# One kernel, its first stage and its heads: head 0's v of half 0 is computed first, two blocks of z behind the first stage, and each head's last chunk is turned in squares

## The chip, the cores and the metric

The kernel runs on one core of a Trainium2 chip. A core has engines with instruction queues of their own, which meet only through semaphores: TensorE (PE; matmuls, with weight loads as PEld), VectorE (DVE), ScalarE (ACT), GpSimd (POOL) and SyncE (SP, which here only issues DMAs). The metric is the device time of one launch in microseconds (us), lower is better. Before the change three runs gave 2084.30, 2090.53 and 2091.62 us.

## The reference

A trunk of two layers over 1024 tokens of width 1024. Only layer 0, gated linear attention with 4 heads, is touched; layer 1 is sparse attention with a top-k.

```python
h = x @ w_in                                    # (1024, 1024) @ (1024, 6160): q, k, v, z, a
g = log_sigmoid(a @ w_a2 + b_a) / 16            # a has 16 columns
# per head, chunk of tokens by chunk:
G = cumsum(g);  q_t = q * exp(G) / 16;  k_t = k * exp(-G)
o = tril(q_t @ k_t.T) @ v + (q * exp(G) / 16) @ S
S = S * decay + k_s.T @ v
# after all heads:
o = o * rsqrt(mean(o * o) + eps) * gn_g         # per head
y = (o * silu(z)) @ w_out
x = layer_norm(alpha * x + y);  x = x + (p @ ple_w) * sigmoid(x @ w_gate)
```

q and k have 256 columns per head, v and z 512. All of it is float32.

## The kernel before

Each float32 operand of a matmul is split into a high part (ScalarE copies it, rounded) and a low part (VectorE subtracts the high part), and each product is three matmuls: high by high, high by low, low by high. A block of 128 output columns over all 1024 inputs and 512 tokens is 24 matmuls of 512 columns. The work is one program order for each engine. The Python code keeps a count of TensorE time (`fl.now`, from the columns of the matmuls that it has written) and a heap of steps with due times; between matmuls it writes the steps that are due into the queues of the other engines. Nothing is reordered on the chip: what is written behind a waiting instruction on an engine waits too.

The tokens are done in two halves of 512. The first stage (`front_phase`) computes q, k and z for both halves in 15 pairs of blocks, with Strassen's seven products in place of eight: `products(1)` to `products(7)` are 12 matmuls each and need sums of parts of x (`T1` to `T5`, made once by `first_sums`, `t3`, `high`, `low`) and of weights (made for each pair by `steps`, `more_steps`, `last_steps`). Such preparing steps stand in `queue`, which `pace` empties by a gap, and which `todo` empties at once where a matmul needs a step. The stage opens with blocks 14 and 15 of z for half 0 (`z_first`), 48 matmuls in plain form, while the sums are made. The second half of x reaches the sums through a copy in DRAM (`xs`, then `load_T`).

Then each half of layer 0 runs. `v_phase(u, X)` computes v of one head, 96 matmuls into four PSUM banks, three of tag `pb` and one called `vT` that shares its bank with `oT`. For half 1 blocks 14 and 15 of z follow the first `v_phase`. Then for each head there is a core (`core_steps`, 16 steps over four chunks of 128 tokens) spread over bulk matmuls, which are the output product of the head before (`out_phase`, 96 matmuls) and v of the head behind (`v_phase`). In a core, `s1(c)` makes the scores (`tr`), `s2(c)` the update of the state (`U`), `s3(c)` the output of the chunk (`o`), and `s4(c)` turns that output and multiplies it by z. There are two ways to turn: by four transposes on TensorE into `oT`, or by squares (`by_square(c)`: 32x32 transposes on VectorE, four DMAs to DRAM and one back in `squares_out`, then `gate`). Before, chunks 0 to 2 of heads 0 to 2 go by squares, and chunk 3 by TensorE; head 3 has two chunks (three in half 1) by squares. A head's loop ends when its `s3(3)` is written (`fl.need(lambda: u.get("late"))`); `out_phase` reads the turned chunks in order.

`g_prep` prepares the next head while a core runs: it loads the gate's weights (`g_load`, on SP), splits them (`g_split`), and `g_phase` does two matmuls into `U` and a chain of ScalarE and VectorE steps on them (absolute value, exponential, logarithm, running sums, two more exponentials), then `qk_phase` multiplies q and k. The first `s1` of a head needs the end of that chain. `Weights` loads and splits plain blocks of weights in the order of `seq`, up to `W.stop`; `W.pace` writes one quarter of a split every 1.15 us of `fl.now`. `split_ahead` splits weights of the later layers in the background.

## Time and profile before

| | us |
|---|---|
| runs | 2084.30, 2090.53, 2091.62 (median 2090.53) |
| the profiled execution | 2087.2 |
| its span, first to last instruction | 2085.1 |
| PE busy | 1940.2 (93%) |
| DVE busy | 1553.6 (75%) |
| ACT busy | 968.8 (46%) |
| mean granted TensorE clock | 0.967 of 2.4 GHz |

TensorE is busy nearly throughout from 1100 us on, and the idle time lies before that. The stages are: the first stage from 0 to about 363.5 us, half 0 of layer 0 to about 640 with its tail to 780, half 1 from there to about 1100, then layer 1. A busy engine in these views may run at the lower clock: a matmul of 512 columns then takes about twice as long. A wait in brackets is the idle time of the engine just before the instruction, and names what ended it.

### The profile page before, as it was taken

What the parts mean: (1) busy time and instruction counts of PE and PEld (TensorE: products, weight loads), DVE (VectorE), ACT (ScalarE), POOL (GpSimd) and SP (SyncE); (2) the same over time, 40 slices, a digit from 0 to 9 for tenths busy, and PEclk for the clock granted to TensorE, in tenths of its full rate; (3) what the DMA queues carried; (4) which work ended last, traced back from release to release, by engine and by line L of the source; (5) the groups of instructions that cost most, each with busy time, mean ns of one, the idle gap of its engine ahead of it and who ended that gap; (6) DMA issues with size and microseconds to landing.
All of it is one profiled execution on the core that took longest, in us unless ns stands there. A gap on an engine that the chain in (4) does not pass through costs nothing.

```text
span 2085.1 us, 26854 instructions
## 1 busy us (share of the span) xinstructions
PE 1940.2 (93%) x8764; PEld 1592.4 (76%) x8764; DVE 1553.6 (75%) x3138; ACT 968.8 (46%) x1852; POOL 304.2 (15%) x568
## 2 busy tenths in 40 slices
PE   7799998878989998789859999999999999999999
PEld 5577887657768887667648888888878888888877
DVE  5677666577788686777886798777779787777873
ACT  3233443555455463444315467676642453434432
POOL 0023333133333202222202000000000000000000
PEclk8899999989999999999979999999999999999999
DMA  5268787889986987678617758887786898888874
GB/s 204 95 241 276 279 280 268 317 271 324 327 308 224 327 276 270 219 275 318 214 58 268 280 166 300 288 275 282 245 302 220 309 341 285 296 300 299 301 290 141
DMA packets 197195, 550.44 MB, mean 264 GB/s; under 512 B 25280, under 2 KB 38592, under 8 KB 190912
## 3 DMA queue, kind: packets, MB, share of 16 engines
q1 hardware_dynamic: 156640, 412.91, 58.0%
q0 software_dynamic: 40416, 135.82, 17.7%
q8 instruction: 69, 1.13, 0.2%
q14 instruction: 70, 0.57, 0.1%
HBM read 359.76 MB, written 190.97 MB: 264 GB/s over the span
## 4 chain that ended last, share of the span: by engine, by line
PE 55%; DVE 10%; DMA 7%; issue 6%; ACT 3%; POOL 1%; SPq 1%; DVEq 0%; ACTq 0%; POOLq 0%
PE pb L59 39%; PE o L59 6%; PE S L59 6%; DMA uf<-od 2%; PE U L59 1%; DMA wa2f<-in_g_a 1%; DMA wlo<-wls 1%; DVE tkj L1122 1%; DMA od<-ot 1%; DVE m L511 1%; DMA wls<-pst 1%; DVE y L811 1%; DVE v L420 1%; DVE bn L855 1%; DVE pst L251 0%
## 5 line engine op out<-in xcount | busy, mean ns | idle before, releaser
L59 PE MATMUL pb<-x,whi 128*128 128x512 f32 x1552 | 487.4, 395 | 11.2 <-DVE v L420 6.1
L59 PE MATMUL pb<-whi,u 128*128 128x512 f32 x1024 | 350.5, 403 | 5.9 <-DVE u L753 2.9
L59 PEld LDWEIGHTS pb<-x,whi 128*128 128x128 f32 x1552 | 286.4, 190 | 66.4 <-DVE v L420 6.5
L59 PE MATMUL pb<-x,wlo 128*128 128x512 f32 x776 | 305.2, 393 | 4.2 <-DVE wlo L1397 4.2
L59 PEld LDWEIGHTS pb<-whi,u 128*128 128x128 f32 x1024 | 198.4, 194 | 50.2 <-DVE u L753 4.3
L59 PE MATMUL pb<-wlo,u 128*128 128x512 f32 x512 | 204.2, 399 | 0.7 <-DMA wlo<-wls 0.7
L59 PEld LDWEIGHTS pb<-x,wlo 128*128 128x128 f32 x776 | 146.9, 189 | 37.8 <-DVE wlo L1397 5.9
L1906 ACT ACTIVATE sq<-P,mx 128x128 f32<-128x128 f32 (+7 forms) x128 | 98.9, 773 | 90.0 <-DVE mx L1899 70.0
L248 ACT ACTIVATE phi<-pst 128x512 fp32r<-128x512 f32 x130 | 81.3, 625 | 117.0 <-DMA pst<-in_d_z 26.4
L59 PE MATMUL pb<-whi,x 128*128 128x512 f32 x384 | 131.1, 395 | 3.8 <-DVE y L811 2.4
L849 POOL TENSOR_SCALAR rstd<-mv 128x1 f32<-128x1 f32 x16 | 5.8, 365 | 842.2 <-DVE mv L858 839.4
L59 PE MATMUL S<-kT,q 128*128 128x512 f32 (+2 forms) x576 | 122.7, 342 | 0.0
L251 DVE TENSOR_TENSOR pst<-pst,phi 128x512 fp32r<-128x512 f32 x130 | 88.8, 683 | 37.6 <-ACT phi L248 37.6
L1952 ACT ACTIVATE ph<-PT 128x512 fp32r<-128x512 f32 (+2 forms) x160 | 86.6, 559 | 65.2 <-PE o L59 43.9
L59 PEld LDWEIGHTS S<-kT,q 128*128 128x128 f32 x576 | 100.7, 188 | 18.4 <-DVE mx L1899 1.2
L59 PEld LDWEIGHTS pb<-wlo,u 128*128 128x128 f32 x512 | 99.1, 194 | 19.7 <-DMA wlo<-wls 1.1
L250 POOL DMA_DIRECT2D whs<-phi x130 | 72.6, 559 | 277.9 <-ACT phi L248 240.3
L253 POOL DMA_DIRECT2D wls<-pst x130 | 71.5, 550 | 260.1 <-DVE pst L251 223.3
L1950 DVE TENSOR_TENSOR PT<-PT,ph 128x512 fp32r<-128x512 f32 (+2 forms) x160 | 93.3, 594 | 20.5 <-ACT ph L1952 20.1
L1166 ACT ACTIVATE tk<-sc,tki 128x768 f16<-128x768 f32 (+2 forms) x90 | 92.8, 1031 | 18.6 <-DVE tki L1175 16.3
L1912 DVE STREAM_TRANSPOSE sq<-sq 128x128 f32<-128x128 f32 (+7 forms) x128 | 97.6, 768 | 3.5 <-ACT sq L1906 3.2
L713 ACT ACTIVATE junk<-o 128x512 bf16<-128x512 f32 x32 | 19.1, 597 | 172.8 <-DVE ot L708 119.0
(425 smaller groups left out, 4379.7 us busy)
## 6 DMA issues: line engine op xcount, KB each, us to landing
whi<-whs SPq DMA_DIRECT2D x160, 512.0 KB
wlo<-wls SPq DMA_DIRECT2D x160, 512.0 KB
sqd<-sq SPq DMA_DIRECT2D x192, 256.0 KB
PT<-sqd SPq DMA_DIRECT2D x48, 1024.0 KB
whs<-phi POOLq DMA_DIRECT2D x130, 256.0 KB, 4.9
wls<-pst POOLq DMA_DIRECT2D x130, 256.0 KB, 5.1
whs<-whi POOLq DMA_DIRECT2D x32, 512.0 KB, 5.5
wls<-wlo POOLq DMA_DIRECT2D x32, 512.0 KB, 6.5
```

The costliest lines, as they stand in the source:

```text
L59: self.pe.matmul(out, lhsT, rhs, start=start, stop=stop)
L248: self.nc.scalar.activation(hi, st.bitcast(F32), AF.Copy)
L250: self.nc.gpsimd.dma_start(there[0][:, c], hi.bitcast(F32))
L251: self.nc.vector.tensor_sub(st, st.bitcast(F32), hi.bitcast(F32))
L253: self.nc.gpsimd.dma_start(there[1][:, c], st.bitcast(F32))
L420: dve.tensor_sub(lo, src, hi.bitcast(F32))
L511: dve.tensor_tensor_scan(m[:, d, cs], m[:, d, cs], ta[:, d, cs], 0.0, op0=OP.add, op1=OP.subtract)
L1166: act.activation(junk()[:, :n], scs[j], AF.Sign, bias=cand[:, j:j + 1].bitcast(F32), accum_out=cnt[:, j:j + 1])
L1906: act.activation(to, rows, AF.Exp, scale=-1.0, bias=mx, accum_out=sm[:, t:t + 1])
L1912: dve.transpose(x, x)
L1950: dve.tensor_sub(lo, lo.bitcast(F32), hi.bitcast(F32))
L1952: chain((0, lambda: act.activation(hi, lo.bitcast(F32), AF.Copy)), (0.8, second))
```

## The change

1. `front_phase` opens with v of head 0 for half 0 (`v_first`, 96 matmuls into four `pb` banks) in place of the two z blocks. v goes to DRAM (`v_s`) and comes back in `v_load` at the start of half 0. The z blocks 14 and 15 now stand at the start of half 0, in banks `o` and `tr`.
2. The second half of x is loaded straight from the input (`xr`, among the first loads). The queue is written anew: the sums `T1` and `T2` are made while `v_first` runs, at a gap of 0.36 and two steps a call, and the weights of the first two pairs behind it. The four small constants and the gate's input weights are loaded elsewhere.
3. At the end of the first stage `last_load` loads two blocks of z early and holds their splits back for 6 us of the count.
4. `by_square(c)` is now true for all four chunks of heads 0 to 2. The cores of heads 1 and 2, and of head 0 in half 0, are spread over 6.5 us less; head 0's core in half 0 starts 5 us into its bulk. Three waiting times in the steps are longer (`ready` by 1.5, `s2` at least 2.0 behind the split of its keys, `s3` 2.6 in place of 1.6).
5. `g_load` moves from SP's queue to POOL's. In half 0 head 0's gate chain starts with the z blocks.

```diff
     for half in range(NH):
         seq += v_keys(0)
-        seq += last_z if half else []
+        seq += last_z
...
-    W.stop = 2
+    W.stop = 4
...
     def g_load(h):
         for i in range(3):
-            nc.sync.dma_start(wa2f[32 * i:32 * i + 16, :], g_a2[:, h * 256:(h + 1) * 256])
+            pool.dma_start(wa2f[32 * i:32 * i + 16, :], g_a2[:, h * 256:(h + 1) * 256])
...
                 if d:
-                    u["ready"] = True
+                    after(1.5, ready)
                     after(0.5, parts)
...
+                fl.ripe(st["kt", c][2] + 2.0)
...
-                fl.ripe(st["At", c] + 1.6)
+                fl.ripe(st["At", c] + 2.6)
...
         def by_square(c):
-            return c < (3 if h < GH - 1 else 2 + half)
+            return h < GH - 1 or c < 2 + half
...
+        def load_r(i, k):
+            nc.sync.dma_start(xr[i][:, k:k + 2],
+                              x_T[4 * i + k:4 * i + k + 2, :, HT:L].rearrange("k p t -> p k t"))
...
-                dve.tensor_sub(t[1], f(T[3][1][:, k]), X.raw[:, k])
+                t[1] = pbank() if k % 2 else room_t()
+                dve.tensor_sub(t[1], xr[0][:, k], X.raw[:, k])
...
+        def v_first():
+            banks = [pbank() for _ in range(4)]
+            for c in range(4):
+                hi, lo = W.take(("v", 0, c))
...
+                    mm(banks[t], xh[:, ts], hi[:, ws], first, False)
+                    mm(banks[t], xh[:, ts], lo[:, ws], False, False)
+                    mm(banks[t], xl[:, ts], hi[:, ws], False, last)
+                    if last:
+                        p = piece()
+                        act.activation(p, banks[t], AF.Copy)
+                        after(1.0, lambda p=p, t=t: nc.sync.dma_start(v_s[t], p))
...
-        xs = dp.tile([NK, 128, HT], F32, name="xs")
-        nc.sync.dma_start(xs, x_T[:, :, later_x])
-        load_T(3, 0)
-        load_T(5, 4)
-        nc.sync.dma_start(wsm, g_a)
-        queue.extend([*a.steps(), *b.steps(), *fills, *(g for k in range(4) for g in first_sums(k)),
-                      *both(t3), *a.more_steps(), *high(3), *low(3), *b.more_steps(), *high(4), *low(4),
-                      *high(5), *a.last_steps(), *low(5)])
-        pacing["due"] = 6.0
+        w4 = [W.step] * 4
+        (s01, r01), (s23, r23) = sums(0), sums(2)
+        queue.extend([put(2), put(3), *w4, *s01, put(4), put(5), *w4, *r01, *s23, put(6), put(7), *w4, *r23])
+        pacing["due"] = 0.5
         fl.pacers.append(pace)
-        fl.run(z_first(14), z_first(15))
+        fl.run(v_first())
+        W.due = 0.0
...
+        queue.extend([*a.steps(), *b.steps(), *fills, *both(t3), *high(3), *low(3), *a.more_steps(), *b.more_steps(),
+                      *high(5), *low(5), room_4, *high(4), *low(4), *a.last_steps()])
...
         def last_load():
-            W.stop = len(W.seq)
+            if W.stop < len(W.seq):
+                W.stop = len(W.seq)
+                W.loads(W.ns + 2)
+                W.due = fl.now + 6.0
...
+    def v_load(u):
+        for t in range(4):
+            vh, vl = t2k("v", F32R), t2k("v", F32R)
+            nc.sync.dma_start(vl.bitcast(F32), v_s[t])
...
             if h == 0:
-                g_prep(u, fl.now + 0.5, 6.0)
-                fl.run(v_phase(u, X))
                 if half:
+                    g_prep(u, fl.now + 0.5, 6.0)
+                    fl.run(v_phase(u, X))
                     for _ in feeder:
                         pass
-                    fl.run(z_last(14, hs), z_last(15, hs))
+                else:
+                    g_prep(u, fl.now, 4.0)
+                    v_load(u)
+                fl.run(z_last(14, hs), z_last(15, hs))
...
-            length = n * B + 15.5
-            spread(steps, fl.now, length)
+            length = n * B + 15.5 - (6.5 if 0 < h < GH - 1 or h == half == 0 else 0.0)
+            spread(steps, fl.now + (5.0 if h == half == 0 else 0.0), length)
```

Three places show how the queues change. The first is VectorE at the start, from the low part of the first piece of x on (`x` are parts of x, `wlo` low parts of weights, `t` and `pb` PSUM tiles of the sums). Before:

```order
L420 TENSOR_TENSOR x<-y,x 128x512 x2
L193 TENSOR_TENSOR wlo<-wst,whi 128x512
L420 TENSOR_TENSOR x<-y,x 128x512 x2
L1369 TENSOR_TENSOR t<-wst 128x512
L1373 TENSOR_TENSOR t<-t,wst 128x512
```

Now:

```order
L193 TENSOR_TENSOR wlo<-wst,whi 128x512 x2
L1313 TENSOR_TENSOR t<-xrh,y 128x512
L1317 TENSOR_TENSOR t<-xrl,t 128x512
L1313 TENSOR_TENSOR pb<-xrh,y 128x512
L1317 TENSOR_TENSOR pb<-xrl,pb 128x512
L420 TENSOR_TENSOR x<-y,x 128x512
L193 TENSOR_TENSOR wlo<-wst,whi 128x512
```

The sums of x (L1313, L1317) now stand between the splits of x and of v's weights, where before the sums of the first pair's weights (L1369) came first.

The second is ScalarE at the end of the first stage, at the last pair's last part (`s4h`; L191 splits plain weights, `pc<-pc` is the silu of a piece of z). Before:

```order
L191 ACTIVATE whi<-wst 128x512
L1458 ACTIVATE pc<-pc 128x512
L191 ACTIVATE whi<-wst 128x512
L1464 ACTIVATE pc<-pb 128x512
L191 ACTIVATE whi<-wst 128x512
L248 ACTIVATE phi<-pst 128x512
L1408 ACTIVATE s4h<-t 128x512
```

Now:

```order
L1485 ACTIVATE pc<-pb 128x512
L248 ACTIVATE phi<-pst 128x512
L1429 ACTIVATE s4h<-t 128x512
L1479 ACTIVATE pc<-pc 128x512
L191 ACTIVATE whi<-wst 128x512 x4
```

Three splits of plain weights stood ahead of `s4h`; now all of them stand behind it.

The third is TensorE at the end of head 1's core in half 0, from the last matmuls of v to the first scores of head 2 (`pb<-whi,u` is the output product, `oT<-ident,ot` the transposes, `tr<-ta,m` the scores). Before:

```order
L59 MATMUL vT<-whi,x 128x512
L59 MATMUL pb<-whi,u 128x512
L59 MATMUL pb<-wlo,u 128x512
L59 MATMUL pb<-whi,u 128x512 x2
L59 MATMUL pb<-wlo,u 128x512
L59 MATMUL pb<-whi,u 128x512
L63 MATMUL oT<-ident,ot 128x128 x4
L59 MATMUL pb<-whi,u 128x512
L59 MATMUL pb<-wlo,u 128x512
L59 MATMUL pb<-whi,u 128x512
L59 MATMUL tr<-ta,m 128x128 x2
```

Now:

```order
L59 MATMUL vT<-whi,x 128x512
L59 MATMUL pb<-whi,u 128x512
L59 MATMUL pb<-wlo,u 128x512
L59 MATMUL pb<-whi,u 128x512 x2
L59 MATMUL pb<-wlo,u 128x512
L59 MATMUL pb<-whi,u 128x512 x2
L59 MATMUL pb<-wlo,u 128x512
L59 MATMUL pb<-whi,u 128x512
L59 MATMUL tr<-ta,m 128x128 x2
```

The transposes are gone. Ahead of these rows, between the output of the core's last chunk and the output product, there now stand 36 matmuls of v where there were 12.

## Rows read from the trace of the kernel before

**Rows 1.** The page: the span, and from its part 1 each engine's busy time, share of the span and number of instructions.

```profile
span 2085.1 us, 26854 instructions
...
PE 1940.2 (93%) x8764; PEld 1592.4 (76%) x8764; DVE 1553.6 (75%) x3138; ACT 968.8 (46%) x1852; POOL 304.2 (15%) x568
```

**Rows 2.** Busy time by stretch: start and end of the stretch, its length, then per engine busy us (and number of instructions), the granted TensorE clock as a share of full speed, the share of the DMA engines that was busy, and GB/s.

```profile
0.00:5.50 5.50, 4.13 (x19) 4.13 (x20) 1.48 (x6) 2.54 (x3) 1.60 (x8) 1.00 0.63 171
...
5.50:26.00 20.50, 17.49 (x63) 12.81 (x61) 11.66 (x18) 10.28 (x17) 0.00 (x0) 0.83 0.85 308
...
45.00:88.50 43.50, 31.61 (x105) 23.02 (x106) 30.41 (x41) 13.66 (x20) 1.28 (x2) 0.80 0.18 66
...
363.50:640.00 276.50, 237.26 (x1041) 193.20 (x1041) 204.62 (x382) 144.40 (x278) 92.86 (x178) 0.93 0.88 312
...
780.00:1100.00 320.00, 260.02 (x1121) 210.03 (x1120) 247.01 (x590) 121.72 (x237) 70.65 (x133) 0.90 0.64 226
```

**Rows 3.** The timeline of TensorE in the first stage: start, duration, engine, line, operation, out<-in, shapes, how many instructions were merged, and in brackets the idle time before and what ended it.

```profile
34.16 0.62 PE L59 MATMUL pb<-x,whi 128*128 128x512 f32 x2
...
34.84 0.62 PE L59 MATMUL pb<-x,whi 128*128 128x512 f32 x2
...
38.57 5.53 PE L59 MATMUL pb<-x,wah 128*128 128x512 f32 x16 [2.90 <-DVE wah L1522]
...
50.66 0.80 PE L59 MATMUL pb<-T2h,whi 128*128 128x512 f32 x1 [2.56 <-ACT T2h L1311]
...
88.54 0.61 PE L59 MATMUL pb<-x,whi 128*128 128x512 f32 x2
```

**Rows 4.** The timeline of VectorE and ScalarE in the same stretch, with the same columns.

```profile
26.91 1.29 DVE L1413 TENSOR_TENSOR wlo<-pst,whi 128x512 fp32r<-128x512 f32 x2
...
37.88 0.31 ACT L1524 ACTIVATE wah<-wsm 128x128 fp32r<-128x128 f32 x1 [7.01 <-DMA wsm<-in_g_a]
...
38.23 0.29 DVE L1522 TENSOR_TENSOR wah<-wsm,wah 128x128 fp32r<-128x128 f32 x1 [4.54 <-ACT wah L1524]
```

**Rows 5.** The timeline of ScalarE, then of TensorE, at the end of the first stage.

```profile
351.79 0.63 ACT L191 ACTIVATE whi<-wst 128x512 fp32r<-128x512 f32 x1 [5.82 <-PE pb L59]
...
357.91 0.63 ACT L191 ACTIVATE whi<-wst 128x512 fp32r<-128x512 f32 x1 [3.96 <-DMA wst<-in_g_v]
...
359.60 0.80 PE L59 MATMUL pb<-T5h,s4h 128*128 128x512 f32 x1 [5.18 <-ACT s4h L1408]
```

**Rows 6.** The timeline of TensorE at the six ends of heads 0 to 2, three in each half: the four transposes of the last chunk into the bank oT, with the wait before them; and two matmuls behind the second of them.

```profile
447.75 1.12 PE L63 MATMUL oT<-ident,ot 128*128 128x128 f32 x4 [5.04 <-DVE v L420]
...
523.57 1.11 PE L63 MATMUL oT<-ident,ot 128*128 128x128 f32 x4 [9.46 <-DVE v L420]
...
524.91 0.63 PE L59 MATMUL pb<-wlo,u 128*128 128x512 f32 x1
...
525.34 0.63 PE L59 MATMUL pb<-whi,u 128*128 128x512 f32 x1
...
595.91 1.12 PE L63 MATMUL oT<-ident,ot 128*128 128x128 f32 x4 [9.47 <-DVE v L420]
...
850.63 1.11 PE L63 MATMUL oT<-ident,ot 128*128 128x128 f32 x4 [7.61 <-DVE v L420]
...
924.97 1.11 PE L63 MATMUL oT<-ident,ot 128*128 128x128 f32 x4 [6.43 <-DVE v L420]
...
995.20 1.12 PE L63 MATMUL oT<-ident,ot 128*128 128x128 f32 x4 [7.65 <-DVE v L420]
```

**Rows 7.** The timeline of VectorE: for three heads the first instructions on the gate's products (m<-U,ba) and the last on the keys (m<-raw,m), which the scores wait for. The first pair is head 1 of half 0, the second head 2 of half 0, the third head 1 of half 1.

```profile
427.43 1.41 DVE L497 TENSOR_SCALAR m<-U,ba 128x512 f32<-128x512 f32 x2 [1.70 <-ACT ta L496]
...
455.87 0.68 DVE L585 TENSOR_TENSOR m<-raw,m 128x512 f32<-128x512 f32 x1
...
499.68 1.41 DVE L497 TENSOR_SCALAR m<-U,ba 128x512 f32<-128x512 f32 x2 [0.77 <-ACT ta L496]
...
520.43 0.68 DVE L585 TENSOR_TENSOR m<-raw,m 128x512 f32<-128x512 f32 x1
...
833.30 1.41 DVE L497 TENSOR_SCALAR m<-U,ba 128x512 f32<-128x512 f32 x2 [0.55 <-ACT ta L496]
...
857.96 1.28 DVE L585 TENSOR_TENSOR m<-raw,m 128x512 f32<-128x512 f32 x2
```

**Rows 8.** A chunk turned in squares in head 2 of half 0, on VectorE: its 32x32 transposes, and the product with z once it has come back by DMA; and SyncE's queue, where two loads of weights are issued.

```profile
535.57 0.71 DVE L708 STREAM_TRANSPOSE ot<-o 128x512 f32<-128x512 f32 x1
...
552.66 0.69 DVE L756 TENSOR_TENSOR uf<-uf,z 128x512 f32<-128x512 f32 x1 [4.08 <-DMA uf<-od]
...
509.54 8.00 SPq L224 DMA_DIRECT2D wst<-in_g_o  x2
```

**Rows 9.** Head 0 of half 0: ScalarE at the gate's weights and at the last reload of its table of functions, and TensorE at the gate's products, at the first scores and at the output of the last chunk.

```profile
375.42 0.42 ACT L478 ACTIVATE w<-wa2f 128x256 fp32r<-128x256 f32 x1 [7.08 <-DMA wa2f<-in_g_a]
...
384.13 1.28 ACT L529 ACT_TABLE_LOAD   x1
...
376.34 0.72 PE L59 MATMUL U<-ah,w 96*128 96x512 f32 x2 [2.55 <-DVE w L420]
...
395.50 1.09 PE L59 MATMUL tr<-ta,m 128*128 128x128 f32 x4 [1.18 <-DVE m L585]
...
436.57 0.79 PE L59 MATMUL o<-v,Al 128*128 128x512 f32 x1 [4.34 <-DVE Al L420]
```

More of the change, by code (lines that the diff above doesn't have):

```diff
@@ L1249, in front_phase, with load_more @@
         load(1, 1)
+        load(2, 2)
         W.loads(2)
-        for k in range(2, NK, 2):
-            load(k, 2)
+        load_r(0, 0)
+        load_r(1, 0)
+        load(4, 2)
+        def load_more():
+            load_r(0, 2)
+            load_r(1, 2)
+            load(6, 2)
+        fl.at(1.9, load_more)
         X.put(0, X.raw[:, 0])
         fl.need(lambda: X.t[0] is not None)
+        for n in range(4):
+            W.reserve(n)
         W.step()
@@ L1259, in front_phase @@
         W.step()
[L1260 to L1269 removed]
+        W.due = 1.0e9
         idle = pp.tile([128, 512], F32, tag="t", name="idle", bufs=2)
@@ L1317, in low, with sums, room_4 @@
                 return g
-            return [t1, t2, high(1), high(2), low(1), t4, low(2)]
+            return [t1, t2, high(1), high(2)], [low(1), t4, low(2)]
+        def sums(k):
+            (a, b), (c, d) = first_sums(k), first_sums(k + 1)
+            return a + c, b + d
         def t3(c):
-            dve.tensor_sub(X.raw[:, 4 + c.start:4 + c.stop], f(T[5][1][:, c]), f(T[3][1][:, c]))
+            fl.need(lambda: all(X.t[4 + k] is not None for k in range(c.start, c.stop)))
+            dve.tensor_sub(X.raw[:, 4 + c.start:4 + c.stop], xr[1][:, c], xr[0][:, c])
         def source(i, c):
-            return {3: X.raw[:, 4 + c.start:4 + c.stop], 4: X.raw[:, c], 5: f(T[5][1][:, c])}[i]
+            return {3: X.raw[:, 4 + c.start:4 + c.stop], 4: X.raw[:, c], 5: xr[1][:, c]}[i]
+        def room_4():
+            T[4] = [fp.tile([128, 4, HT], F32R, tag=f"T4{n}", name=f"T4{n}") for n in "hl"]
         def high(i):
@@ L1492, in front_phase @@
         queue = deque()
-        pacing = {"due": 0.0, "gap": 0.9}
+        pacing = {"due": 0.0, "gap": 0.36}
         def one():
@@ L1505, in pace @@
                 one()
+                if queue and now >= pacing["due"]:
+                    pacing["due"] += pacing["gap"]
+                    one()
         P = [Pair(n) for n in range(len(pairs))]
         a, b = P[:2]
-        def z_first(block):
-            def ev(ps):
-                t = piece()
-                act.activation(t, ps, AF.Silu)
-                after(1.0, lambda: nc.sync.dma_start(z_s[block, :, 0:HT], t))
-            return fm_block(("z", block), X, ev)
+        def v_first():
+            banks = [pbank() for _ in range(4)]
+            for c in range(4):
+                hi, lo = W.take(("v", 0, c))
+                if c == 1:
+                    a.load()
+                    nc.sync.dma_start(wsm, g_a)
+                if c == 3:
+                    b.load()
+                order = [(t, kk) for t in range(4) for kk in range(2)]
+                if c == 0:
+                    order.sort(key=lambda x: x[1])
+                for t, kk in order:
+                    ts = slice(t * 128, t * 128 + 128)
+                    todo(lambda: ("x", 2 * c + kk) in made)
+                    xh, xl = X[2 * c + kk]
+                    ws = slice(kk * 512, kk * 512 + 512)
+                    first, last = c == 0 and kk == 0, c == 3 and kk == 1
+                    mm(banks[t], xh[:, ts], hi[:, ws], first, False)
[5 more added lines that the diff above has]
+                        after(1.0, lambda p=p, t=t: nc.sync.dma_start(v_s[t], p))
+                    yield
         wsm = fp.tile([128, NK, 16], F32, name="wsm")
@@ L1625, in trunk_kernel @@
     pool.memset(wa2f, 0.0)
-    R = [lp.tile([128, 2, 512], F32, name=f"R{h}") for h in range(GH)]
-    sc0 = lp.tile([128, 896], F32, name="sc0")
+    R = []
     def g_prep(u, start, gap):
```

68 lines of the change are left out of this document (37 added, 31 removed).

## Prediction

> **What bounds the kernel now.** I read the page first: TensorE is busy for 1940.2 of 2085.1 us [rows 1], so a change can win idle time of TensorE, or time at its lower clock, and little else. The view by stretches says where that lies. Up to 88.5 us TensorE waits for its operands: from 45.0 to 88.5 it is busy for 31.61 of 43.5 us, at a granted clock of 0.80, while the DMA engines are busy for 0.18 of that time, so the data is there by then and it is the steps on VectorE and ScalarE that are late [rows 2]. Half 0 of layer 0 has 276.5 - 237.3 = 39 us of idle TensorE, and the stretch of half 1 has 320 - 260 = 60 us [rows 2]. The timelines then say who ended each wait.
>
> In the first stage the sums of x are late because of a queue. ScalarE stands 7.01 us for a small load (`wsm`), VectorE 4.54 us behind it, and only then do the sums begin [rows 4]; the load stands on SP behind the copy of x through DRAM. TensorE pays with 2.90 us at `wah`, 2.56 at T2 and more like them [rows 3]. At the stage's end ScalarE stands at splits of v's weights, 5.82 us for a buffer and 3.96 for a load, and `s4h`, which stands behind them on ScalarE, costs TensorE 5.18 [rows 5]. In layer 0 the largest waits are the six at `oT`: 5.04, 9.46, 9.47, 7.61, 6.43, 7.65, together 45.7 us [rows 6]. The transposes of a head's last chunk need the bank that v of the next head was made in, and the split of that v comes late on VectorE.
>
> Two rates are needed. At full clock three matmuls take 34.84 - 34.16 = 0.68 us, 0.227 each [rows 3]. Behind a long wait two start 0.43 us apart [rows 6], which is 1.2 GHz in place of 2.4. So a wait costs its length and then half the time until the clock is back.
>
> **A, the opening: -22 us.** At 88.54 us TensorE starts on the third pair [rows 3]. It has then done 48 matmuls of z, 16 of the gate and 156 of the first two pairs, and `b` lacks its last 12. With 96 matmuls of v in place of 48 the same point has 48 x 0.227 = 10.9 us more of work in front of it, which leaves the later stage: moved work costs nothing in itself.
> When is the new point reached? First the loads. 171 GB/s for 5.5 us are 0.94 MB, and then 308 GB/s flow [rows 2]. Ahead of the last quarter of x stand 5.5 MB in the new order and ahead of v's fourth block 6.0 MB, so they are there at 5.5 + 4.56/0.308 = 20 and 22 us, and with some 2 us to land (an estimate) at 22 and 24. Then VectorE: two 512-column steps in a row take 1.29 us, so one takes 0.60 [rows 4], and a 1024-column step twice that (an estimate). Behind the load of v's third block come 6 remaining steps of the sums, 4 new ones, and the low parts of x and v: the last quarter of v's matmuls starts at about 27.5 and, partly at the lower clock, ends at about 35. VectorE is then free of v at 29.4, has 6 steps of sums left (33.0), and 7 + 8 steps for the weights of the first two pairs (42). TensorE can finish `products(1)` and `(2)` of both at 47.6 and the gate at 51. T1 and T2 are long made, and T3, T5, T4 follow on VectorE at about 48, 56 and 59, ahead of TensorE each time. 156 - 48 = 108 matmuls, 24.5 us, and 1 or 2 us of waits bring the point to 77. The win is 88.5 + 10.9 - 77 = 22 us. If the loads flow badly or the lower clock lasts, the win is 12; if v's fourth block isn't late, 30. The third pair's own waits stay.
>
> **B, the end of the first stage: -7.** In the new order no split of plain weights stands ahead of `s4h`. The 5.18 us go, and half of the some 3.5 us at the lower clock behind them. What hides the loads now is the last pair's matmuls. From 0, where another wait takes the place, to -9.
>
> **C, head 0 of half 0: +7.** Its stretch had waits of 2.55 at U, 1.18 at the first scores, 4.34 at `Al` [rows 9] and 5.04 at `oT` [rows 6]. Now the chain from U to the first scores has the same 71 matmuls (16 us) in front, but it shares ScalarE with the silu of z and the splits of the v that came back. Before, it took 395.50 - 376.34 = 19.2 us, so 3 to 4 us of wait are due there. In the trace ScalarE loads its table of functions in 1.28 us [rows 9]; the new order has one load more in the chain, for the silu of z15 between the logarithm and the next exponential. The Trainium skill says under "ScalarE: Activation LUTs", section "Table sets: the hidden batching unit", that calls should be batched by set; the change goes against that. By that rule the loss would be the whole 1.28 us, where I count about 1, since ScalarE would wait here for VectorE's sums in part.
> The end of this head is the dear part. v is used up before the core ends, so the last core steps stand close together and 36 matmuls of the output product (8.2 us) follow at once. They need chunks 1 and 2 back from DRAM. A chunk in squares took 552.66 - 535.57 = 17.1 us from its transposes to its product with z [rows 8], and some 3 us go to the output ahead and the splits behind. Chunk 2 is needed 3.6 + 2 + 5.4 = 11 us behind its output, so TensorE stands for about 9, then 2 for the keys, and 5 in the close steps of head 1 (estimates, by the 4.34 at `Al`). With some 5 us at half speed the region loses about 33 us where it lost 26. Between -3 and +15.
>
> **D, ends of heads 1 and 2 in both halves: -21.** The waits of 9.46, 9.47, 6.43 and 7.65 [rows 6] are 33.0 us; about 4 us at the lower clock behind each cost 2 each, so 41 us hang on these four. The transposes go. What is late next? First the scores of the next head. Their chain took 520.43 + 0.68 - 499.68 = 21.4 us [rows 7], and in front of them 93 matmuls now stand in half 0 and 92 in half 1 (21 us), where it was 74 and 76. VectorE no longer has splits of v inside that chain. That wait is 0 to 2 us. Second, the fourth chunk in the output product: it is needed some 84 matmuls, 19 us, behind its output, and is back after 17 to 21. That is 0 to 3 us, and more where SP stands at a load of weights, as for 8.00 us [rows 8]. I take 5 us of loss for each end in all, 20 of 41. From -36 to -10.
>
> **E, the end of head 0 in half 1: -2.** Its core isn't shortened. The chain had taken 857.96 + 1.28 - 833.30 = 25.9 us [rows 7]; now 71 matmuls (16 us) stand in front of the scores, so 5 to 8 us of the wait of 7.61 [rows 6] come back there. From -8 to +6.
>
> **F, -2:** six times four transposes leave TensorE, at 1.1 us of lower clock [rows 6], part of which is counted in D. The gate's weights on POOL instead of SP cost nothing where POOL is free; head 0 waited 7.08 us for them on SP [rows 9], so they bound nothing new, 2 us to either side.
> The Trainium skill, "DMA: Bandwidth & Descriptors", section "Issuing engine by pattern", gives simple loads to Sync, whose descriptors are made by hardware, and calls that path generally faster. That speaks against this edit; no row here times such a load on POOL, and the sum does not use it.
>
> The sum is -22 - 7 + 7 - 21 - 2 - 2 = -47 on the profiled execution's 2087.2, so 2040. That execution is 3.3 us below the median of the runs shown; I forecast 2041. Layer 1 and the end of half 1 stay.
>
> **Rivals.**
> 1. The squares only move the wait: a fourth chunk comes back late at every end, D and E win nothing and C stays. For it: chunks needed 17 us and more, VectorE itself stood 4.08 us for one [rows 8]. Against it: the 19 us of matmuls that now lie between. Time: 2087 - 22 - 7 + 7 = 2065.
> 2. The opening is bound by loads, so TensorE starves at v's blocks, and A wins 5 in place of 22: 2057. For it: 8 MB in the first 30 us at 308 GB/s. Against it: x's second half no longer goes through DRAM, 4 MB of traffic less.
> 3. Slower. Each of the six ends has one square more on SP's queue. Where SP stands 8 us for a buffer of weights [rows 8], the square waits, VectorE stands at its product with z, and behind it on VectorE stand the keys and the splits of v and weights. Price: a return of 17 us and SP's stand of 8 twice is 33, of which 19 are covered; 14 and some 5 at half speed are 19 for each end, where D has 10 now. Six ends lose 9 more each, 54, and A and B win 29: 2087 - 29 + 54 = 2112. It decides where the end's loss exceeds 10 + 29/6 = 15, a return of 29 us. Head 1 of half 0 shows a chain of 455.87 + 0.68 - 427.43 = 29.1 us [rows 7], a case of that kind; the others show 21 to 26.
> 4. The parts work but cancel, with C at +15 and the rest at the weak ends: about 2080.
>
> **How the numbers follow.** The forecast has 0.60 (2015 to 2055), rival 1 0.13, rival 2 0.12, rival 3 0.06, rival 4 0.09. Half a per cent, about what a measurement of this kernel can tell from no change, is 10 us: faster means below 2080. The forecast and rivals 1 and 2 lie there, as does a little of rival 4: 0.86 faster, 0.08 same, 0.06 slower. The range for 8 in 10 leaves out rival 3, most of rival 4 and the best tail: 2015 to 2073.
>
> **What would show it.** A: the third pair's first matmul at about 77 us, with v's 96 in front, and no long wait at T2. B: no wait at `s4h`. C: waits of TensorE in the output product of head 0, ended by `u`. D: no `oT` before head 3, and waits under 4 us around the first scores and the fourth chunk of heads 1 and 2. It would be wrong if VectorE's waits for `uf<-od` grew to 8 us and more, if TensorE stood at v's blocks before 35 us for more than 10 us in all, or if the granted clock of half 0 were not above 0.93.

## The result, and the profile after

The changed kernel takes 2073.62 us (median of 12 runs, 2068.13 to 2081.37), the kernel before 2091.11 (12 runs, 2084.30 to 2096.74): a ratio of 0.9921, 95% interval 0.9903 to 0.9940. It is faster by 17 us, where 50 were forecast, and lies just above the range. The profiled execution took 2080.34 us, 6.7 above its median, so a single pair of traces carries several us that are chance. What follows rests on stretches of traces for places, and on medians for sizes; where a size is read from a trace, the text says so.

The page of the changed kernel, its span and the first line of part 1, answers to [rows 1]:

```profile
span 2078.6 us, 26899 instructions
...
PE 1944.5 (94%) x8740; PEld 1593.8 (77%) x8740; DVE 1554.8 (75%) x3138; ACT 974.0 (47%) x1858; POOL 314.9 (15%) x592
```

The busy time by stretch, with the columns of [rows 2]:

```profile
5.50:26.00 20.50, 15.62 (x59) 11.77 (x59) 12.07 (x19) 8.00 (x15) 3.41 (x6) 0.92 1.01 379
45.00:88.50 43.50, 41.61 (x176) 33.56 (x175) 32.36 (x44) 15.69 (x24) 1.11 (x2) 0.96 0.28 93
...
345.00:640.00 295.00, 249.25 (x1039) 199.72 (x1038) 212.00 (x393) 147.07 (x280) 96.34 (x183) 0.90 0.85 300
780.00:1100.00 320.00, 265.22 (x1125) 213.81 (x1124) 246.90 (x579) 125.09 (x239) 75.13 (x145) 0.89 0.65 229
```

The opening did what it says: from 45 to 88.5 us TensorE is busy for 41.61 us in place of 31.61, at a clock of 0.96 in place of 0.80. The heads did not: their clock is 0.90 and 0.89, against 0.93 and 0.90 in [rows 2] (from 363.5 to 640 us, the stretch of [rows 2], it is 0.90 too). That was one of the three signs of being wrong that the prediction gave; the other two did not come.

TensorE's timeline at the places that the forecast spoke of: the waits in v's product, the third pair's first matmul (86.04, in [rows 3] at 88.54), the first matmul behind the first stage (350.43), and the ends of heads 1 and 2 in both halves, where [rows 6] had the waits for `oT`.

```profile
21.87 0.69 PE L59 MATMUL pb<-whi,x 128*128 128x512 f32 x1 [4.56 <-ACT whi L191]
...
32.73 0.79 PE L59 MATMUL pb<-whi,x 128*128 128x512 f32 x1 [3.29 <-ACT whi L191]
...
86.04 0.61 PE L59 MATMUL pb<-x,whi 128*128 128x512 f32 x2
...
350.43 0.62 PE L59 MATMUL zp<-x,whi 128*128 128x512 f32 x2
...
509.32 0.79 PE L59 MATMUL pb<-whi,u 128*128 128x512 f32 x1 [5.51 <-DVE v L420]
510.34 1.05 PE L59 MATMUL pb<-whi,u 128*128 128x512 f32 x2
...
584.44 0.80 PE L59 MATMUL pb<-whi,u 128*128 128x512 f32 x1 [5.87 <-DVE v L420]
...
915.85 0.50 PE L59 MATMUL pb<-whi,u 128*128 128x512 f32 x1 [4.45 <-DVE v L420]
...
981.94 0.79 PE L59 MATMUL pb<-whi,u 128*128 128x512 f32 x1 [3.55 <-DVE v L420]
```

No transpose waits any more at these four ends; the output product does, for a `pb` bank, until a split of the same v frees it. Behind the waits the clock is lower: the two matmuls merged at 510.34 take 1.05 us, those at 86.04 take 0.61. How late that split is, ScalarE and VectorE show at the end of head 1 in half 0, first ScalarE, then VectorE:

```profile
500.35 0.60 ACT L717 ACTIVATE junk<-o 128x512 bf16<-128x512 f32 x1 [5.71 <-DVE ot L712]
...
501.06 1.28 ACT L529 ACT_TABLE_LOAD   x1
```

```profile
497.74 1.28 DVE L526 TENSOR_TENSOR m<-m,mid 128x512 f32<-128x512 f32 x2
...
499.61 0.71 DVE L712 STREAM_TRANSPOSE ot<-o 128x512 f32<-128x512 f32 x1
501.96 0.69 DVE L760 TENSOR_TENSOR uf<-uf,z 128x512 f32<-128x512 f32 x1 [1.65 <-DMA uf<-od]
...
506.11 0.68 DVE L585 TENSOR_TENSOR m<-raw,m 128x512 f32<-128x512 f32 x1
...
508.58 0.68 DVE L420 TENSOR_TENSOR v<-pb,v 128x512 fp32r<-128x512 f32 x1
...
517.61 0.69 DVE L760 TENSOR_TENSOR uf<-uf,z 128x512 f32<-128x512 f32 x1
...
521.45 0.69 DVE L757 TENSOR_TENSOR u<-uf,u 128x512 fp32r<-128x512 f32 x1
```

ScalarE stands 5.71 us at the sum of squares until VectorE has copied the same bank; that copy stands behind the gates' subtraction, and the gates' exponentials stand behind the sum. VectorE waits for a square to come back, multiplies the keys, and only then splits v. The last two rows are the last chunk itself, which was copied at 499.61: its product with z, and its last split.

### The profile page after: what moved, and what is told of

Same layout as the page of the kernel before. It is cut to its first block, busy times and chain, and to the rows that moved or that the text cites. A ratio compares the mean times of both kernels' runs of the same rounds, so it can differ in the third digit from the quotient of the medians.

```text
span 2078.6 us, 26899 instructions
## 1 busy us (share of the span) xinstructions
PE 1944.5 (94%) x8740; PEld 1593.8 (77%) x8740; DVE 1554.8 (75%) x3138; ACT 974.0 (47%) x1858; POOL 314.9 (15%) x592
## 4 chain that ended last, share of the span: by engine, by line
PE 51%; DVE 10%; issue 10%; DMA 7%; ACT 3%; POOL 2%; SPq 0%; DVEq 0%; POOLq 0%; ACTq 0%
PE pb L59 37%; PE o L59 6%; PE S L59 6%; DMA od<-ot 1%; PE U L59 1%; DVE tkj L1126 1%; DMA wlo<-wls 1%; DMA wls<-pst 1%; DVE y L815 1%; DVE m L511 1%; DMA uf<-od 1%; DMA pst<-in_d_o 1%; DMA wa2f<-in_g_a 1%; DVE bn L859 1%; DMA pst<-in_d_z 1%
## 5 line engine op out<-in xcount | busy, mean ns | idle before, releaser
L59 PE MATMUL pb<-x,whi 128*128 128x512 f32 x1488 | 463.9, 393 | 2.4 <-DVE x L420 1.2
L59 PE MATMUL pb<-whi,u 128*128 128x512 f32 x1024 | 358.2, 411 | 50.3 <-DVE v L420 21.0
L59 PEld LDWEIGHTS pb<-x,whi 128*128 128x128 f32 x1488 | 272.9, 189 | 52.9 <-DVE x L420 2.3
L59 PE MATMUL pb<-x,wlo 128*128 128x512 f32 x744 | 291.6, 392 | 4.2 <-DVE wlo L1418 4.1
L59 PEld LDWEIGHTS pb<-x,wlo 128*128 128x128 f32 x744 | 140.0, 188 | 37.1 <-DVE wlo L1418 6.6
L59 PE MATMUL pb<-whi,x 128*128 128x512 f32 x400 | 138.9, 406 | 13.4 <-ACT whi L191 7.9
L59 PEld LDWEIGHTS pb<-whi,x 128*128 128x128 f32 x400 | 78.3, 196 | 32.0 <-ACT whi L191 8.9
L1170 ACT ACTIVATE tk<-sc,tki 128x768 f16<-128x768 f32 (+2 forms) x90 | 92.8, 1031 | 18.3 <-DVE tki L1179 16.0
```

Of the source, the lines that this page charges most:

```text
L59: self.pe.matmul(out, lhsT, rhs, start=start, stop=stop)
L1170: act.activation(junk()[:, :n], scs[j], AF.Sign, bias=cand[:, j:j + 1].bitcast(F32), accum_out=cnt[:, j:j + 1])
```

## The experiments

All sizes are medians over several runs, and each ratio is against the kernel before on the same chip. Runs from different chips are best compared by their ratios; 0.001 is 2.1 us.

The theory at the outset: the opening is worth what the traces show, and the last part (squares of the last chunks, shorter cores, longer waits) loses. The rival: the heads gain as forecast, and something else eats the opening.

**The two parts alone.** e1 takes the last part out of the changed kernel:

```diff
-            return h < GH - 1 or c < 2 + half
+            return c < (3 if h < GH - 1 else 2 + half)
...
-                    after(1.5, ready)
+                    ready()
...
-                fl.ripe(st["kt", c][2] + 2.0)
...
-                fl.ripe(st["At", c] + 2.6)
+                fl.ripe(st["At", c] + 1.6)
...
-            length = n * B + 15.5 - (6.5 if 0 < h < GH - 1 or h == half == 0 else 0.0)
+            length = n * B + 15.5 - (6.5 if h == half == 0 else 0.0)
```

> The new opening, the z blocks and head 0's shorter core, with the heads' ends as they were before (three chunks in squares, cores 6.5 us longer, the old waits). Theory: the opening is worth what the two traces show (24 us by the end of the first stage, 7.5 us given back in head 0, 4 us won at head 0 of half 1), and the squares of each head's last chunk with the shorter cores lose some 9 us; so this kernel takes 2091 - 24 + 7.5 - 4 = 2070 us, some 3 to 9 us below the changed kernel's 2074. Rival: the heads' ends gain the 20 us of the forecast and something else eats the opening; then this kernel takes 2085 to 2095 us.

Measured 2058.06 us, ratio 0.9843 (0.9819 to 0.9866). The opening alone wins 34 us, 12 more than I expected, and the last part costs 16 of them.

e2 is the kernel before with the last part alone: the lines above the other way round, and for the cores

```diff
-            length = n * B + 15.5
+            length = n * B + 15.5 - (6.5 if 0 < h < GH - 1 else 0.0)
```

> The kernel before with the last part alone: every chunk of heads 0 to 2 in squares, cores of heads 1 and 2 shorter by 6.5 us, the longer waits. Theory: the wait at a head's end is only moved, from the bank oT to the bank that the next head's v holds, so 2091 to 2100 us. Rival: as forecast, 2091 - 21 = 2070 us.

Measured 2095.04, ratio 1.0018 (1.0006 to 1.0031). The forecast's 21 us are not there. But it costs 3 us here and 16 on the new opening; why the parts don't add stays open.

**What in the last part costs.** e3 gives the changed kernel's cores of heads 1 and 2 their 6.5 us back.

```diff
-            length = n * B + 15.5 - (6.5 if 0 < h < GH - 1 or h == half == 0 else 0.0)
+            length = n * B + 15.5 - (6.5 if h == half == 0 else 0.0)
```

> The changed kernel with the 6.5 us given back to the cores of heads 1 and 2 (four cores). Their next head's gate chain then starts 0.74 x 6.5 = 4.8 us later. Theory: the chain from the gates to v's splits is what the output product's bank waits for, so each of the four waits (5.5, 5.9, 4.5, 3.6 us) grows by up to 4.8 us: 2074 + 4 x 4.8 = 2093 us at most, above 2080 at least. Rival: the waits are made by the crowding that the shorter cores bring; then they shrink and it takes 2060 to 2072 us.

Measured 2085.31, ratio 0.9970 (0.9957 to 0.9983): 12 us slower than the changed kernel. The size fits the theory; the waits that it named do not: from 345 to 640 us the waits for v's bank fell from 11.4 to 2.7 us, and those for the first scores rose from 9.0 to 21.5. It is one chain, and which of its users is late depends on the order.

e5, e6 and e7 add one piece each to e1.

```diff
# e5: squares
-            return c < (3 if h < GH - 1 else 2 + half)
+            return h < GH - 1 or c < 2 + half
# e6: shorter cores
-            length = n * B + 15.5 - (6.5 if h == half == 0 else 0.0)
+            length = n * B + 15.5 - (6.5 if 0 < h < GH - 1 or h == half == 0 else 0.0)
# e7: waits
-                    ready()
+                    after(1.5, ready)
...
+                fl.ripe(st["kt", c][2] + 2.0)
...
-                fl.ripe(st["At", c] + 1.6)
+                fl.ripe(st["At", c] + 2.6)
```

> Run e1 (the opening alone, 2058 us) with one thing added: the last chunk of heads 0 to 2 in squares as well. Theory after e1 and e3: the squares are the costly part. In the trace of the changed kernel, head 0's output product stands 4.7, 2.8 and 4.0 us for its chunks while VectorE stands 4.8 us at the product's first add with head 1's q and k queued behind it; in e1 the transposes through TensorE come later in its order and nothing waits for a chunk. So 2058 + 15 to 27 = 2073 to 2085 us, with waits of the output product for u. Rival: the longer waits in the planner (e7) cost it and the squares alone do not: 2055 to 2064 us.

> Run e1 with one thing added: the cores of heads 1 and 2 shorter by 6.5 us, squares as before. The gate chain of the next head starts 4.8 us earlier. Theory: in e1 each of these ends still shows a wait of 6 to 9 us for the bank oT, which v's last split holds behind the gate chain; an earlier chain frees it up to 4.8 us earlier at four ends: 2058 - 8 to 19 = 2039 to 2050 us. Rival: the shorter core brings its q and k products onto VectorE before they can be done and the wait changes its name only: 2054 to 2064 us.

> Run e1 with one thing added: the planner's three longer waits (1.5 us until a head is ready, 2.0 us from the split key to the state product, 2.6 for 1.6 us from the scores to the output). They move matmuls of other work ahead, and cost nothing of themselves. Theory: within 4 us of e1, 2054 to 2062 us. Rival: they put each head's first scores behind more of the output product and are what the last part costs: 2068 to 2075 us.

| | us | ratio (95%) | against e1 |
|---|---|---|---|
| e5, squares | 2076.21 | 0.9929 (0.9902 to 0.9956) | +18 |
| e6, shorter cores | 2048.97 | 0.9800 (0.9775 to 0.9825) | -9 |
| e7, waits | 2059.71 | 0.9843 (0.9817 to 0.9869) | 0 to 2 |

So on e1 the squares cost, the shorter cores win and the longer waits do nothing, each size as the theory had it. The pieces are not independent, though: 18 - 9 + 0 is 9, and the last part costs 16. e3, which is also e5 with the longer waits, fills the gap. It takes 9 us more than e5 (ratios 0.9970 and 0.9929, intervals 0.9957 to 0.9983 and 0.9902 to 0.9956, which just part), so the longer waits cost nothing without the squares and some 9 us with them. From there the shorter cores give 12 back, to the changed kernel: 18 + 9 - 12 = 15. Why the waits hurt only beside the squares was not tested. In e6 the wait for v partly changes its name, as its rival said: from 345 to 1100 us the waits at `oT` fall from 46.5 us in e1 to 16.4, and those for a `pb` bank of v rise from 1.1 to 18.0.

TensorE's waits from 345 to 640 us (line, what ended them: us in total, times, longest), first of e1, then of e5:

```profile
PE oT L63 <- DVE v L420: 22.1, 3, 8.9
PE tr L59 <- DVE m L585: 11.6, 3, 7.1
```

```profile
PE tr L59 <- DVE m L585: 28.4, 6, 9.2
PE pb L59 <- ACT u L753: 9.9, 4, 3.6
PE pb L59 <- DVE u L756: 3.6, 4, 2.0
```

The squares remove 22.1 us at `oT` and bring 13.5 for `u` and 16.8 more for the first scores. The sums are not far apart, but the waits are more (39 in place of 21 from 345 to 1100 us). Two stretches from the first matmul of z to the end of head 3's core, and from head 0's first scores in half 1 to the wait in front of the first `xt`, e1 and then e5:

```profile
349.50:609.00 259.50, 219.82 (x960) 179.34 (x960) 194.31 (x365) 137.73 (x265) 90.55 (x172) 0.92 0.89 313
770.00:1039.80 269.80, 234.55 (x1025) 191.23 (x1024) 206.51 (x483) 106.03 (x211) 70.23 (x135) 0.94 0.71 248
```

```profile
345.90:618.00 272.10, 224.07 (x950) 179.80 (x949) 195.09 (x365) 138.39 (x265) 91.55 (x172) 0.91 0.87 302
780.00:1055.50 275.50, 240.50 (x1010) 192.87 (x1009) 205.80 (x480) 105.82 (x210) 70.28 (x135) 0.92 0.71 247
```

e5 is 18.3 us longer here (547.6 against 529.3). Idle time is 8.1 of it (83.0 - 74.9). The other 10.2 us are busy time, with 25 matmuls fewer, at a granted clock of 0.91 and 0.92 where e1 has 0.92 and 0.94: more of them ran at the lower clock. Less work took more time.

How late a square is, head 1's last chunk in half 0 of e5 shows, TensorE and then VectorE:

```profile
499.74 0.76 PE L59 MATMUL tr<-ta,m 128*128 128x128 f32 x2 [7.46 <-DVE m L585]
...
514.90 0.50 PE L59 MATMUL pb<-whi,u 128*128 128x512 f32 x1 [3.01 <-ACT u L753]
```

```profile
491.23 0.69 DVE L759 TENSOR_TENSOR uf<-uf,z 128x512 f32<-128x512 f32 x1 [1.34 <-DMA uf<-od]
...
492.50 0.71 DVE L711 STREAM_TRANSPOSE ot<-o 128x512 f32<-128x512 f32 x1
...
512.88 0.68 DVE L759 TENSOR_TENSOR uf<-uf,z 128x512 f32<-128x512 f32 x1
...
515.08 0.68 DVE L756 TENSOR_TENSOR u<-uf,u 128x512 fp32r<-128x512 f32 x1
```

From its transposing copy to its last split the chunk takes 515.08 + 0.68 - 492.50 = 23.3 us, and the copy itself stands behind a wait for the third chunk's return. In e1 the same chunk takes 18.3 by TensorE, 488.55 to 506.83, although the transposes wait 8.95 us in it.

**Is it lateness?** e12 writes the last chunk's read and gate earlier in e5:

```diff
-                after(5.5, lambda: gate(c, uf))
-            after(3.5, squares_in)
+                after(4.5 if c == 3 else 5.5, lambda: gate(c, uf))
+            after(2.0 if c == 3 else 3.5, squares_in)
```

> Run e5 with the last chunk's square read back and gated 2.5 us earlier in the planner's order (1.5 us at the read, 1.0 at the gate). Theory of lateness: the waits for u at six heads' ends shrink by up to 2.5 us each and the clock holds longer behind them: 2060 to 2070 us. Rival: the read back has not landed then, VectorE stands at it with the gate chain queued behind: 2075 to 2083 us.

Measured 2067.37, ratio 0.9891 (0.9870 to 0.9912): 8 to 9 us of the 18 are back, by ratios and by medians, with intervals that just overlap e5's. The waits for `u` from 345 to 1100 us fall from 36.3 us in e5 to 29.3. That speaks for lateness, as the theory says, for about half of the cost; what the rest is, no run here shows.

**Is it ScalarE's stand?** e4 (on the changed kernel), e8 (on e1), e10 (on e6) and e11 (on e5) write the sum of squares ahead of the copy (the swap):

```diff
+                junk = lp.tile([128, 512], BF16, tag="junk", name="junk")
+                act.activation(junk, ps, AF.Square, accum_out=u["ss"][:, c:c + 1])
                 if by_square(c):
                     dve.transpose(ot.rearrange("p (m b i) -> p b m i", m=4, b=4), ps)
...
-                junk = lp.tile([128, 512], BF16, tag="junk", name="junk")
-                act.activation(junk, ps, AF.Square, accum_out=u["ss"][:, c:c + 1])
```

> The changed kernel with ScalarE's sum of squares written ahead of VectorE's transposing copy of the same bank, in every chunk; same work. Theory: at a head's last chunk ScalarE no longer stands 5.7 us behind VectorE's copy (itself queued behind the gates' subtraction), so its table load and exponentials come 2 to 3 us earlier, the bank waits shrink by as much at four ends: 2074 - 8 to 12 = 2062 to 2066 us. Rival: VectorE's queue alone sets the time of v's last split, or the copy that now comes 0.8 us later delays the squares: 2072 to 2078 us.

> Run e1 with the sum of squares written ahead of the copy of the same bank (as in e4). In the changed kernel it brought 2.8 us, inside the two intervals. Theory: the scores' last copy of each head stands behind the next head's gate chain on VectorE in e1 too, and ScalarE stands behind it: 2 to 6 us less, 2052 to 2056 us. Rival: the transposes through TensorE need that copy early, and its delay by 0.8 us costs as much as ScalarE wins: 2057 to 2061 us.

> Run e6 with the sum of squares ahead of the copy (as in e4 and e8, which gained 2.8 and 2.7 us). Theory: ScalarE's stand behind VectorE's copy is on the gate chain at each head's end; 2 to 4 us less than e6, 2045 to 2047 us. Rival: with shorter cores the chain has other limits: 2048 to 2051 us.

> Run e5 (the opening with all chunks of heads 0 to 2 in squares, 2076 us) with the sum of squares ahead of the transposing copy. In e5's trace ScalarE stands 7.4 us at head 1's end for that copy, which on VectorE stands behind a wait for the third chunk's square to be read back; the gates' exponentials are queued behind. Theory: this stand is about half of what the squares cost: 2064 to 2070 us. Rival: the squares cost by their lateness, TensorE standing for the last chunks (36 us of waits for u in e5, 4 in e1): 2072 to 2078 us.

| with the swap | us | ratio (95%) | us without the swap |
|---|---|---|---|
| e4 | 2070.81 | 0.9896 (0.9879 to 0.9914) | 2073.62 |
| e8 | 2055.37 | 0.9832 (0.9808 to 0.9856) | 2058.06 |
| e10 | 2044.10 | 0.9773 (0.9749 to 0.9797) | 2048.97 |
| e11 | 2074.50 | 0.9925 (0.9903 to 0.9947) | 2076.21 |

Each wins 2 to 5 us by the medians (2 to 6 by the ratios, under 1 for e11), inside overlapping intervals; four of one sign speak for some 3. The 8 to 12 us of e4 and the half of the squares' cost of e11 fall: ScalarE's stand is long, but it is not what ends the chain. That VectorE's queue does is e4's rival, which the size fits.

**With all helps.** e14 is e12 with e6's cores and the swap; it differs from e10 in the squares and their early return alone.

> Run e12 (squares of the last chunks, read back early, 2067 us) with the shorter cores of e6 and the sum of squares ahead as in e10. Theory: the squares still come later than TensorE can use them; the shorter cores are worth 9 us here too and the sum of squares nothing: 2056 to 2060 us, 12 us or more over e10. Rival: with all these helps the squares come in time and their missing transposes win: 2040 to 2046 us, as e10 or below.

Measured 2057.36, ratio 0.9850 (0.9832 to 0.9869), against e10's 0.9773: 13 to 16 us. The squares of the last chunks lose here with every help that was tried. e10 has the lowest median of all, though its interval overlaps e6's; it beats the kernel before by 2.3%, and the changed one. Its interval lies clear of e8's, which has the longer cores, so the shorter cores are a gain here too (11 to 12 us).

**The opening.** e9 moves the splits of x and v ahead of the sums in e6:

```diff
-        queue.extend([put(2), put(3), *w4, *s01, put(4), put(5), *w4, *r01, *s23, put(6), put(7), *w4, *r23])
+        queue.extend([put(2), put(3), *w4, put(4), put(5), *w4, put(6), put(7), *w4, *s01, *r01, *s23, *r23])
```

> Run e6 (the opening with shorter cores, 2049 us) with one thing moved: in the opening's queue for ScalarE and VectorE, the splits of x's blocks 4 to 7 and of v's third and fourth weight blocks now stand ahead of all sums of halves, instead of between them. TensorE's own order is unchanged. Theory: in v's product TensorE waits 1.6 and 4.1 us for these splits, not for loads: ScalarE had stood 3.4 and 6.4 us behind VectorE's sums just ahead of them. Both waits go, and some of the half-clock run behind them (0.74 of full between 20 and 40 us); the sums still end before the pairs' products need them. 4 to 8 us less: 2041 to 2045 us. Rival: the loads of these blocks land just as late, or the sums are now late for the pair products; the waits change their names: 2047 to 2052 us.

Measured 2055.51, ratio 0.9828 (0.9805 to 0.9850): not faster than e6, 6 us slower by the medians, with intervals that overlap. My theory fell. ScalarE's timeline in e9, the stretch of the loads, and the two DMA queues up to 25.6 us (packets, MB, share) show why:

```profile
25.60 1.15 ACT L428 ACTIVATE x<-y 128x512 fp32r<-128x512 f32 x2 [5.21 <-DMA y<-in_x_T]
28.09 1.15 ACT L191 ACTIVATE whi<-wst 128x512 fp32r<-128x512 f32 x2 [1.34 <-DMA wst<-in_g_v]
```

```profile
5.50:25.60 20.10, 17.16 (x73) 13.25 (x73) 7.42 (x12) 6.18 (x12) 3.42 (x6) 1.00 1.03 388
```

```profile
q1 hardware_dynamic: 2926, 6.30, 69.6%
q0 software_dynamic: 648, 2.39, 22.8%
```

With nothing in front of them the last quarter of x is there at 25.60 and v's last weights at 28.09; TensorE still waits 2.2 and 2.6 us in v's product, and then 6.9 for the first pair's weights, since the sums come late. So in e9 the loads set v's product, and the order of e6 hid the sums behind them. By the end of the first stage the two traces are 0.5 us apart (349.9 in e6, 350.4 in e9), so the 6 us of the medians have no place that these traces show.

**The banks of z.** e13 takes z's own banks out of e1:

```diff
-        return fm_block(("z", block), X, ev,
-                        bank=lambda: pp.tile([128, 512], F32, tag=("o", "tr")[block % 2], name="zp"))
+        return fm_block(("z", block), X, ev)
```

> Run e1 (the opening alone, 2058 us) with z's last two blocks of each half in the banks of the other products again. Theory: ahead of head 0 of half 1 TensorE again stands some 6 us for a bank that v's last splits hold, as it did before (6.1 us at pb<-x,whi), and half 0 loses 0 to 2 us: 2064 to 2066 us. Rival: the 8.7 us that head 0 of half 1 gained come from elsewhere: 2056 to 2060 us.

Measured 2063.14, ratio 0.9874 (0.9852 to 0.9897), 5 us more by the medians, with intervals that overlap. TensorE's waits from 740 to 800 us have one line, and e1 has none there:

```profile
PE pb L59 <- DVE v L420: 5.5, 1, 5.5
```

From head 3's first scores in half 0 to head 0's in half 1 the trace takes 206.5 us, as before (206.6), and 198.0 in e1. So 8 us at this place are the banks', by the traces; by the medians 5.

## Why the forecast failed, by its steps

- **A (-22): the mechanism was right, the size was off.** The point came at 86.04 with 48 more matmuls in front: 88.54 + 10.9 - 86.04 = 13.4 us, near the weak end given (12). This trace is one of the late ones: in the 13 traces with this opening the point lies between 80.6 and 86.2 us, so A is worth 13 to 19. What was mis-sized is the way to the last quarter of v's matmuls, which starts at 32.73 in place of 27.5. ScalarE gets the weights of v's third block at 21.18 and then stands for VectorE's sums:

```profile
21.18 1.15 ACT L191 ACTIVATE whi<-wst 128x512 fp32r<-128x512 f32 x2 [1.40 <-DMA wst<-in_g_v]
28.70 0.60 ACT L1324 ACTIVATE T1h<-t 128x512 fp32r<-128x512 f32 x1 [6.37 <-DVE t L1317]
```

  The term behind it is the loads: "with some 2 us to land ... at 22 and 24". In e9, where no sums stand in front, the data came at 25.6 and 28.1, although the DMA engines moved more than I counted on, 388 GB/s in place of 308. By 25.6 us 8.7 MB had moved, where I had 5.5 MB ahead. 2.4 MB of that went over POOL's queue: v's split weights, which are written to DRAM for half 1 (`whs`, `wls`) and which my count left out. SP's queue had moved 6.3 MB, with loads issued behind x among them. Rival 2 had this mechanism at a worse price. The rest of the 9 us to 77 came behind v: waits of 1.21 and 1.81 us and matmuls at the lower clock, which put the end of `products(1)` and `(2)` at 57.9 in place of 47.6.
- **B (-7): right in its mechanism.** There is no wait at `s4h`. From the third pair to the end of the first stage the kernel gains 364.4 - 350.4 - (88.5 - 86.0) = 11.5 us, and e1's trace 9.6; the forecast's best end was 9. The end before is this row:

```profile
364.43 0.39 PE L59 MATMUL pb<-whi,x 128*128 128x512 f32 x1
```

- **C (+7): near in size, but not by the squares alone.** From the end of the first stage to head 1's first scores the traces take 91.4 us now and 91.1 before, with some 34 matmuls fewer (7.7 us), so about 8 us are lost. The waits are those that were named: the output product of head 0 stands 4.67, 2.75 and 4.01 us for `u`. The extra table load came too: head 0's chain has four loads of 1.28 us on ScalarE (359.7, 363.7, 367.2, 370.2), where it had three. But the squares by themselves do not make the loss, as the runs with one piece each show (us from the end of the first stage, and the matmuls in between, each from one trace):

| | to head 1's first scores | to head 2's first scores |
|---|---|---|
| e1 | 80.5 (227) | 152.0 (461) |
| e5, squares | 78.1 (227) | 153.8 (460) |
| e7, longer waits | 95.2 (254) | 155.6 (460) |
| e3, both | 91.3 (239) | 159.9 (460) |
| the changed kernel | 91.4 (240) | 162.9 (462) |

  The longer waits put more matmuls in front of head 1's scores, and up to head 2 neither piece costs over 4 us alone; together they cost 8. Why they do is open.
- **D (-21): wrong, and the step that failed.** The question "What is late next?" was answered with two users, the first scores and the fourth chunk, and the third was put at nothing without a reason: the output product, which needs the `pb` banks that the next head's v holds. "VectorE no longer has splits of v inside that chain" is where it got lost. The splits now stand behind the keys, so the keys come in time (the chain takes 17.9 to 20.2 us, and no first scores of heads 2 and 3 wait), and the output product waits for the splits instead (5.51, 5.87, 4.45, 3.55). Taking the transposes away handed their wait on. "Back after 17 to 21" was wrong too. Head 1's last chunk in half 0 is split 27 us behind its output (ends 495.5, split 522.1), and the output product comes to it just then. That no wait for `u` shows there is luck: the wait for v's bank has used the time up. In e5, whose cores are not shortened, some 55 large matmuls stand in between where 84 were counted, the chunk is split 28 us behind its output (ends 487.5, split 515.8), and TensorE does stop for it. By the two traces D comes to a loss of 8 us in place of the 21 won, counted from head 1's first scores to head 3's with the matmuls made equal. These are the stretches of half 0 and half 1, first of the changed kernel, then of the one before:

```profile
441.81:587.17 145.36, 124.16 (x514) 100.28 (x515) 102.57 (x191) 70.42 (x137) 51.39 (x98) 0.89 0.82 288
846.84:984.66 137.82, 122.91 (x514) 98.89 (x513) 102.55 (x239) 55.51 (x110) 34.59 (x68) 0.92 0.77 272
```

```profile
455.50:596.82 141.32, 119.07 (x534) 97.67 (x535) 105.94 (x196) 71.27 (x139) 53.15 (x99) 0.94 0.90 322
858.70:996.11 137.41, 119.97 (x530) 97.56 (x531) 104.99 (x247) 57.16 (x113) 35.76 (x68) 0.96 0.79 276
```

  The four waits are 13.6 us shorter than the four at `oT` (19.4 for 33.0), but the idle time falls by 3.6 us only (39.7 to 36.1), since others take their place: 4.01 and 3.11 for `u` of head 0, 4.08 for a bank of the output product. And TensorE is busy 8.0 us longer with 36 matmuls fewer, at a clock of 0.89 and 0.92 in place of 0.94 and 0.96. The 5 us of loss that the forecast allowed for each end did not cover that. Rival 1 was the nearer story, at 2065; rival 3 had the lateness.
- **E (-2): nothing to be seen at its place.** From head 0's first scores in half 1 to head 1's the changed kernel takes 56.9 us with 9 matmuls (2.0 us) more than before (55.2), and e1 55.3. A gain lies ahead of that, in z's banks, an edit that I had priced at nothing: 8.6 us in e1's trace, 3.9 in the changed kernel's.
- **F** can't be told apart at its size.

Summed over e1's own trace, with the third pair at 83.20: A 16.2, B 9.6 and the banks 8.6 are 34.4 us, of which other stretches give 5.5 back; the trace gains 28.9 in all and the medians say 34. The last part gives 16 of that back. The forecast's 2041 needed a gain in the heads; with the shorter cores alone added to e1, 2049 was there to be had.

## What to carry to other kernels

When a wait is removed by taking away its instruction, look for the next user of what releases it: here the late splits of one v released the transposes' bank and the output product's. Price a detour through memory by its whole return in the queues of the kernel, not by its engine time: the 24 transposes that left TensorE were replaced by returns like the one of 23 us in e5. Test an edit of several pieces piece by piece, and then in pairs: the shorter cores were a gain that the squares hid, and the longer waits were free alone and cost some 9 us beside the squares.

## What was not expected of the hardware

A wait's length is not its price. e1 and e5 idle 75 and 83 us in the same stretches; the busy time, at the lower clock for longer (0.91 and 0.92 against 0.92 and 0.94), makes more of the difference (10.2 us) than the idle time (8.1). From 345 to 1100 us 39 waits break up TensorE's work in e5, and 21 in e1. That the number of the waits makes the difference is not shown, since no run varies it alone.

ScalarE's sum of squares, which only reads a bank, stood for VectorE's copy, which only reads it too, at 31 of 32 chunks, 28 in squares and 3 in plain copies:

```profile
L717 ACT ACTIVATE junk<-o x32: 597/597/598, 390.5 to 1024.9; 128x512 bf16<-128x512 f32 x32
...
  DVE ot L712: 148.1, 28
  DVE ot L715: 11.4, 3
```

The Trainium skill, "PSUM — Partial Sum Buffer", section "PSUM bank collisions raise a hardware error", says that two engines reading one bank collide as a write and a read do, and that accesses are therefore put in an order. The trace agrees that the two never overlap, in all 32 chunks of the changed kernel, and ScalarE idles 159.5 us in front of its reads; the swap (e4, e8, e10, e11) brings only 2 to 5 us, so most of that time was free.
